# Two of three down-projection parts of a feed-forward block as seven half-sized products

## The chip, the core and the metric

The kernel runs on one core of a Trainium2 chip. The core's engines run side by side, each in the order of its own list of instructions, and wait for one another through semaphores: TensorE (PE) for matrix products, VectorE (DVE) for elementwise work and reductions, ScalarE (ACT) for activations and copies, GpSimd (POOL) and SyncE (SP), which here mostly start transfers. The metric is the device time of one execution in microseconds (us), and the number compared is the median of several runs.

## The reference, cut to what matters

Two layers run one after the other over 512 tokens of width 1024. Each has a token-mixing sublayer and then the feed-forward block that is changed here:

```
def _swiglu(x, w_gate, w_up, w_down):
    h = silu(einsum('bsd,df->bsf', x, w_gate)) * einsum('bsd,df->bsf', x, w_up)
    return einsum('bsf,fd->bsd', h, w_down)

for l in range(2):
    mix = _hybrid_mixer(x, ...)
    x = _layer_norm(ALPHA * x + mix, ln1_g[l], ln1_b[l])
    ffn = _swiglu(x, w_ffn_gate[l], w_ffn_up[l], w_ffn_down[l])
    x = _layer_norm(ALPHA * x + ffn, ln2_g[l], ln2_b[l])
```

The inner width of the block is 2816, that is 22 feature tiles of 128. All arrays are float32.

## The kernel before

**Products in three pieces.** A float32 operand is kept as a high part (a copy that ScalarE rounds to the matmul type) and a low part (the rest, subtracted on VectorE); `hilo` makes the two. Every product of two operands is three matmuls: high by high, high by low, low by high. In the names, `whi` and `wlo` are the parts of a weight, `xh`/`xl` those of the block's input, `ht` those of `h`, `raw` is a weight as loaded, `sn` a working tile, `ps` and `px` are accumulators in PSUM, and `xtok` holds the residual stream of all 512 tokens.

**Seven products instead of eight.** Where two matrices can be cut into 2 by 2 blocks, `tall` and `wide` multiply them by Winograd's form of Strassen's scheme: seven products of half-sized blocks, from sums of blocks of the left side (S1 to S4) and of the right side (P1 to P4). `ORDER` lists the seven as (number, left block, right block). Their results are added in chains of one accumulator: products 1, 6, 7 and 4 go one after the other into chain A, product 2 into chain X, 5 and 3 into chain C. Between two products of a chain the sum so far is read out, because each stage of the chain is a result of its own; the next product may not add to the accumulator before that read. The class `Right` loads the weight blocks; P1 and P3 are made by an accumulating transfer that POOL starts, P2 and P4 by an addition on VectorE in place. Weights' high and low parts lie in two sets of four buffers (`wp`), loaded weights in eight (`rawp`).

**The block before the change.** The 22 feature tiles are worked off in three parts, `FPARTS`, of 6, 8 and 8. In a part, `ffn_plain` (the very first pair) or `ffn_pair` makes two feature tiles of `h` at a time; a pair is seven products of 24 matmuls on 256 columns. Then the part's share of the down projection is added to `xtok`: for each of two halves of 512 output columns, `xstat` runs over the part's feature tiles and four token tiles, three matmuls of 512 columns for each. These are 24 matmuls a feature tile, 528 a layer. Loaded rows of the down weights are split into high and low once and used for all tokens, and `residual` adds each finished accumulator into `xtok`.

**The end of a layer.** In the second half of the last part the four token tiles are taken one after the other (`token_outer`), and `norm` normalizes each as soon as it is complete: statistics, a power on POOL, a refinement, and two passes over 1024 columns on VectorE. In the first layer the normalized tile is also transposed on TensorE (`to_xT`) and split into `xh` and `xl`, which the next layer's first products need; in the second it goes to the output.

**What sets the order.** The program is written as one stream, and a list scheduler orders each engine's instructions by priority and its own guess of when operands are there; pieces of other work are handed in between matmuls by `tick`. Engines then run that fixed order. The order outside the feed-forward block and the first products behind it is the same before and after the change.

Of the kernel before, what the change touches and what calls it, by code (L numbers as in the profile page):

```python
# [11 lines left out]
F32 = mybir.dt.float32  # L12
# [3 lines left out]
ALU = mybir.AluOpType  # L16
# [31 lines left out]
L0, L1 = 383, 255  # L48
WARM = 3
BK = 32  # L50
FPARTS = ((0, 6), (6, 14), (14, 22))


@with_exitstack
def hybrid_kernel(ctx, tc, x, rel_bias, w_in, b_in, w_attn_proj, w_ret_proj, w_out,
# [23 lines left out]
    def stage(name, bufs=1, side="left"):  # L79
        return tc.tile_pool(name=name, bufs=bufs, side=side, reuse_waits="tile")  # L80
# [604 lines left out]
    def layer(ly, cp):  # L685
# [470 lines left out]
        g_, b_ = (fp.tile([P, D], F32, name=n) for n in ("lng", "lnb"))  # L1156
        stats = [sm.tile([P, 2, 6], F32, tag=f"stats{i}", name="stats", bufs=1) for i in range(NI)]

        def ln_par(gsrc, bsrc):
            pool.dma_start(g_, gsrc.partition_broadcast(P))  # L1160
            pool.dma_start(b_, bsrc.partition_broadcast(P))

        def norm(i, dst=None):
            xi = xt[:, i]
            mv = sm.tile([P, 2], F32, tag="mv", name="mv")
            dve.bn_aggr(out=mv, in_=stats[i])
            rs = rstd_of(mv[:, 1:2])
            dve.scalar_tensor_tensor(out=xi, in0=xi, scalar=mv[:, 0:1], in1=g_, op0=ALU.subtract, op1=ALU.mult)
            n = D if dst is None else D // 2
            for c in range(0, D, n):  # L1170
                o_ = xi[:, c:c + n]
                dve.scalar_tensor_tensor(out=o_, in0=o_, scalar=rs, in1=b_[:, c:c + n], op0=ALU.mult, op1=ALU.add)  # L1172
                if dst is not None:
                    nc.sync.dma_start(dst[:, c:c + n], o_)
# [65 lines left out]
        final = ly == DEPTH - 1  # L1240
        cp = []

        def ffn_plain(f, o_):

            ug, uu = pair_units(wg_l, f * P), pair_units(wu_l, f * P)
            pgs = wstat_halves([(u, e) for u in (ug, uu) for e in range(2)])
            drain()
            side.extend(x_sums(xc))
            pace(8)
            for e in range(2):  # L1250
# [3 lines left out]
                hilo(t, o_[:, 0, e], o_[:, 1, e])  # L1254

        def ffn_pair(f, o_):

            sn = {}

            def put(v, ts_):  # L1260
                hilo(v, o_[:, 0, :, ts_], o_[:, 1, :, ts_])

            def ev(i, ps):
                p2 = ps.rearrange("p (q t) -> p q t", q=2)
                if i in (1, 5, 6):
                    sn[i] = work("sn").rearrange("p (q t) -> p q t", q=2)
                    act.copy(out=sn[i], in_=p2)
                elif i == 2:
                    dve.tensor_tensor(out=sn[1], in0=p2, in1=sn[1], op=ALU.add)
                elif i == 3:  # L1270
                    v = sn[6]
                    dve.tensor_tensor(out=v, in0=p2, in1=v, op=ALU.subtract)
                    act.activation(out=v, in_=v, func=AF.Silu)
                    dve.tensor_tensor(out=v, in0=v, in1=sn[1], op=ALU.mult)
                    put(v, slice(0, 256))
                elif i == 7:
                    dve.tensor_tensor(out=sn[5], in0=sn[5], in1=p2, op=ALU.subtract)
# [8 lines left out]
        for part, (f0, f1) in enumerate(FPARTS):  # L1286
            ht = []
            for f in range(f0, f1, 2):
                ht.append(fo.tile([P, 2, 2, S], F32R, tag="op", name="ht"))
                (ffn_pair if f else ffn_plain)(f, ht[-1])  # L1290
                if f == 2:
                    drain()
                    ln_par(ln2_g[ly], ln2_b[ly])

            def h_tok(k, i, ht=ht):
                t, q = ht[k // 2], k % 2
                return t[:, 0, q, i * P:(i + 1) * P], t[:, 1, q, i * P:(i + 1) * P]

            last = part == len(FPARTS) - 1
            rate[0], credit[0] = 0.5 / STEP, 0.0  # L1300
            for hf in range(2):
                def evd(i, ps, hf=hf, part=part, last=last):
                    residual(i, hf, ps, part == 0, last)
                    if last and hf == 1:
# [6 lines left out]
                tail = last and hf == 1  # L1311
# [65 lines left out]
```

## Time and profile before

| | |
|---|---|
| median of three runs | 2134.78 us (2132.10 to 2138.97) |
| the profiled execution, its own time | 2133.13 us |
| its span, first to last instruction | 2131.3 us |
| mean granted TensorE clock | 0.999 |
| busy: PE / DVE / ACT / POOL | 2113.2 / 1488.1 / 1060.9 / 239.5 us |
| down projection, first layer: first matmul on `ht`, first matmul of the last half, last `norm` | 784.6, 1043.8, 1077 us |
| down projection, second layer: first matmul of the last half, last matmul | 2100.4, 2121.9 us |

A row of a timeline gives the start in us, the duration in us, the engine, the line of the program, the operation, the output and inputs with their shapes, how many instructions are merged, and in brackets how long the engine stood idle before it and what ended that. In grouped rows the figures behind the bar are the busy time in us and the mean in ns of one instruction, and then the idle time before them. Matmuls overlap, so the distance from one start to the next, not the duration, is what one costs; VectorE's instructions overlap by less than 0.1 us.

### The profile page before, as it was taken

The numbers are of one execution on the slowest core, as the hardware profiler recorded it, in microseconds if no ns is written. First come the engines' busy times: TensorE is split into PE (matmuls) and PEld (weight loads), VectorE is DVE, ScalarE is ACT, GpSimd is POOL, SyncE is SP. The second block draws the span as 40 slices with busy tenths as digits, with TensorE's granted clock in tenths as the row PEclk, the third lists the DMA queues.
The fourth block names the chain that finished last, engine by engine and source line by source line (L and its number), as shares of the span: only waits on it lengthen the run. The fifth ranks groups of instructions, "written<-read, shape, count | busy, mean of one in ns | idle before, by whom it ended". The sixth has DMA issues, their size and how long they took to land.

```text
span 2131.3 us, 34718 instructions
## 1 busy us (share of the span) xinstructions
PE 2113.2 (99%) x13914; PEld 1917.3 (90%) x13914; DVE 1488.1 (70%) x2113; ACT 1060.9 (50%) x1641; POOL 239.5 (11%) x249
## 2 busy tenths in 40 slices
PE   9999999999999999999999999999999999999998
PEld 8989888889988999989899898888899889999996
DVE  7666888786734776747687578887867358675575
ACT  5567655556623354525255665555665234444350
POOL 4111111101000100000120111101000001010001
PEclk9999999999999999999999999999999999999999
DMA  8866466777776266656258555758687672666551
GB/s 243 213 160 150 124 154 177 181 187 177 242 252 193 60 169 148 168 129 163 76 156 226 144 128 131 194 137 217 158 204 252 211 198 59 179 140 177 120 157 40
DMA packets 313410, 351.32 MB, mean 165 GB/s; under 512 B 22045, under 2 KB 251585, under 8 KB 313120
## 3 DMA queue, kind: packets, MB, share of 16 engines
q1 hardware_dynamic: 227712, 253.01, 38.7%
q0 software_dynamic: 58256, 83.29, 21.1%
q10 hardware_dynamic: 27280, 12.80, 2.1%
q8 instruction: 109, 1.79, 0.3%
q14 instruction: 53, 0.43, 0.1%
HBM read 323.26 MB, written 28.53 MB: 165 GB/s over the span
## 4 chain that ended last, share of the span: by engine, by line
PE 89%; issue 4%; DVE 3%; ACT 2%; DMA 1%; POOL 1%; POOLq 0%; DVEq 0%; ACTq 0%
PE ps L83 81%; PE px L83 6%; DVE wlo L359 1%; PE px L584 1%; PE px L1042 1%; ACT whi L353 1%; ACT s L574 1%; DMA exd<-pk 1%; PE px L192 1%; POOL ry L134 0%; DVE xtok L1172 0%; DMA raw<-in_w_in 0%; DVE raw L375 0%; PE px L649 0%; DMA mb<-exd 0%
## 5 line engine op out<-in xcount | busy, mean ns | idle before, releaser
L359 DVE TENSOR_TENSOR wlo<-raw,whi 128x1024 fp32r<-128x1024 f32 (+1 forms) x462 | 536.8, 1165 | 267.0 <-ACT whi L353 262.5
L353 ACT CAST whi<-raw 128x1024 fp32r<-128x1024 f32 (+1 forms) x462 | 460.7, 1002 | 461.8 <-PE ps L83 252.0
L83 PE MATMUL ps<-xs,whi 128*128 128x256 f32 (+1 forms) x2944 | 572.2, 293 | 0.4 <-ACT sn L814 0.4
L83 PEld LDWEIGHTS ps<-xs,whi 128*128 128x128 f32 x2944 | 467.5, 191 | 15.1 <-issue 1.7
L83 PE MATMUL ps<-xs,wlo 128*128 128x256 f32 (+1 forms) x1472 | 430.2, 292 | 0.6 <-DVE wlo L359 0.6
L83 PE MATMUL ps<-xh,whi 128*128 128x256 f32 (+1 forms) x1424 | 422.7, 299 | 1.9 <-ACT xh L94 1.4
L83 PE MATMUL ps<-xh,wlo 128*128 128x256 f32 (+1 forms) x1424 | 418.6, 295 | 1.0 <-DVE wlo L95 1.0
L83 PE MATMUL ps<-xl,whi 128*128 128x256 f32 (+1 forms) x1424 | 419.5, 295 | 0.0
L83 PEld LDWEIGHTS ps<-xs,wlo 128*128 128x128 f32 x1472 | 281.7, 191 | 6.1 <-DVE wlo L359 1.1
L83 PEld LDWEIGHTS ps<-xh,whi 128*128 128x128 f32 x1424 | 271.0, 191 | 15.3 <-ACT xh L94 2.8
L83 PEld LDWEIGHTS ps<-xl,whi 128*128 128x128 f32 x1424 | 272.2, 191 | 8.3 <-DVE xl L95 0.6
L83 PEld LDWEIGHTS ps<-xh,wlo 128*128 128x128 f32 x1424 | 271.9, 191 | 7.5 <-DVE wlo L95 1.2
L95 DVE TENSOR_TENSOR wlo<-raw,whi 128x1024 fp32r<-128x1024 f32 (+2 forms) x108 | 125.5, 1163 | 167.8 <-ACT whi L94 167.4
L83 PE MATMUL ps<-whi,xs 128*128 128x512 f32 (+1 forms) x768 | 225.0, 362 | 1.0 <-ACT sn L498 1.0
L94 ACT CAST whi<-raw 128x1024 fp32r<-128x1024 f32 (+2 forms) x108 | 107.8, 1001 | 211.6 <-PE ps L83 137.3
L83 PE MATMUL ps<-whi,ht 128*128 128x512 f32 x576 | 178.4, 389 | 0.0
L344 POOL DMA_DIRECT2D raw<-in_w_in x80 | 98.8, 1261 | 691.1 <-DMA raw<-in_w_in 224.0
L375 DVE TENSOR_TENSOR raw<-raw 128x1024 f32<-128x1024 f32 (+1 forms) x132 | 154.3, 1169 | 7.3 <-DMA raw<-in_w_in 5.0
L83 PEld LDWEIGHTS ps<-whi,xs 128*128 128x128 f32 x768 | 137.8, 188 | 20.5 <-ACT sn L498 1.3
L83 PE MATMUL ps<-wlo,xs 128*128 128x512 f32 (+1 forms) x384 | 138.2, 360 | 0.1
L344 POOL DMA_DIRECT2D raw<-in_w_ffn_gate x40 | 51.8, 1294 | 682.1 <-DMA raw<-in_w_ffn_up 239.3
L83 PEld LDWEIGHTS ps<-whi,ht 128*128 128x128 f32 x576 | 108.1, 188 | 22.4
(207 smaller groups left out, 2895.3 us busy)
## 6 DMA issues: line engine op xcount, KB each, us to landing
raw<-in_w_in SPq DMA_DIRECT2D x168, 512.0 KB, 5.3
raw<-in_w_in POOLq DMA_DIRECT2D x64, 512.0 KB, 8.3
raw<-in_w_ffn_up SPq DMA_DIRECT2D x64, 512.0 KB, 4.1
raw<-in_w_ffn_gate SPq DMA_DIRECT2D x44, 512.0 KB, 4.7
raw<-in_w_ffn_down SPq DMA_DIRECT2D x44, 512.0 KB, 3.9
raw<-in_w_ffn_gate POOLq DMA_DIRECT2D x40, 512.0 KB, 6.7
raw<-in_w_ret_proj SPq DMA_DIRECT2D x32, 512.0 KB, 6.3
raw<-in_w_in SPq DMA_DIRECT2D x56, 256.0 KB, 4.8
```

Source lines behind the costliest of these rows:

```text
L83: pe.matmul(ps, lhsT=a, rhs=b, start=start, stop=stop, skip_group_check=True)
L94: act.copy(out=hi, in_=src)
L95: dve.tensor_tensor(out=lo, in0=src, in1=hi.bitcast(F32), op=ALU.subtract)
L192: pe.transpose(px[:, d * P:(d + 1) * P], src[:, (4 * hf + d) * P:(4 * hf + d + 1) * P], ident)
L344: pool.dma_start(r, self.src({"P1": "B12", "P3": "B22"}[n], u), accum_op=ALU.add)
L353: act.copy(out=h, in_=src)
L359: dve.tensor_tensor(out=l, in0=src, in1=h.bitcast(F32), op=ALU.subtract)
L375: dve.tensor_tensor(out=r, in0=r, in1=self.t["B22" if n == "P2" else "B21", u], op=ALU.add)
L574: act.activation(out=s[:, hh, n0:], in_=s[:, hh, n0:], func=AF.Exp, bias=m_, scale=-1.0, accum_out=l_)
L584: pe.transpose(px[:, hh, j * P:(j + 1) * P], ss[od][:, hh, j * P:(j + 1) * P], ident)
L1042: pe.transpose(px[:, t * P:(t + 1) * P], ys[i][:, t * P:(t + 1) * P], ident)
```

## The change

`FPARTS` becomes 8, 8 and 6. The down projection of the first two parts is done by `tall` in its seven-product form (`down_blocks`): the left blocks are `h` with 256 tokens by the four even or four odd feature tiles, the right blocks are the down weights of the even or odd tiles by 512 columns. Tokens are stationary and weights stream, as before. Each product has two token tiles, four feature tiles and three matmuls of 512 columns, which makes 24, and 168 a part. The last part, of six tiles, keeps the old form.

For that, `h` is stored as seven blocks (A11, A12, A22, S1 to S4) with high and low parts. `h_sums` makes S1 to S4 for each pair of feature tiles by four additions of 256 columns on VectorE. A part's 14 pieces of the right side have a high copy and a low subtraction each, four additions for P2 and P4, and four accumulating transfers for P1 and P3; the ten loads and those four transfers stand where eight loads stood. Products 5, 6 and 7 are copied out of PSUM on ScalarE and then added to `xtok`, the others are added from PSUM: 14 additions a part where there were eight. The layer norm's scale and shift lie in other tiles, and those of the second norm are loaded after the last pair.

```diff
-FPARTS = ((0, 6), (6, 14), (14, 22))
+FPARTS = ((0, 8), (8, 16), (16, 22))
+HB = {"A11": 0, "A12": 1, "A22": 2, "S2": 3, "S3": 4, "S4": 5, "S1": 6}
...
-        fo = fin.enter_context(stage("fo", 5))
+        fo = fin.enter_context(stage("fo", 4))
...
+        def h_put(o_, v, c, step):
+            e = c + step * (v.shape[1] - 1) + 1
+            hilo(v, o_[:, c:e:step, 0], o_[:, c:e:step, 1])
+
+        def h_sums(o_, a11, a12, a21, a22):
+            h_put(o_, a22.unsqueeze(1), HB["A22"], 1)
+            dve.tensor_tensor(out=a22, in0=a21, in1=a22, op=ALU.subtract)
+            dve.tensor_tensor(out=a21, in0=a11, in1=a21, op=ALU.subtract)
+            dve.tensor_tensor(out=a11, in0=a22, in1=a11, op=ALU.subtract)
+            dve.tensor_tensor(out=a12, in0=a11, in1=a12, op=ALU.add)
...
-                    put(v, slice(256, 512))
+                    if sums:
+                        h_sums(o_, v0[:, 0], v0[:, 1], v[:, 0], v[:, 1])
+                        h_put(o_, v, HB["S3"], 2)
+                        h_put(o_, v0, HB["S2"], 2)
+                    else:
+                        h_put(o_, v, 2, 1)
...
+        def down_blocks(f0, f1, ht, first):
+            nk = (2,) * ((f1 - f0) // 4)
+
+            def src(b, u):
+                k = f0 + (b[1] == "2") + 4 * u
+                c = (b[2] == "2") * 512
+                return wd_l[:, k:k + 3:2, c:c + 512]
+
+            def left(an, j, ts_):
+                t = ht[j][:, HB[an], :, ts_]
+                return t[:, 0], t[:, 1]
...
+            def ev(i, a, ps):
+                v = ps
+                if i in (5, 6, 7):
+                    v = work("sn")
+                    act.copy(out=v, in_=ps)
...
+            run(tall(Right(src, [(n, 512) for n in nk]), 512, left, ev))
...
+            if not last:
+                down_blocks(f0, f1, ht, part == 0)
+                continue
+            lt = fo.tile([P, 2 * D], F32, tag="op", name="lnp")
+            ln_par(lt, ln2_g[ly], ln2_b[ly])
```

**VectorE at the start of a part's down projection.** In the first layer, changed kernel, from the last instruction that needs the last product of the pair (L1301): `ht_8099` is the part's last pair, `wlo_8374` a low part of the second product's weights, `wlo_8407` and `wlo_8410` those of the third, `ps_8376` and `ps_8390` the two halves of chain A.

```order
L1301 TENSOR_TENSOR sn_8176<-sn_8176,ps_8119 128x512
L360 TENSOR_TENSOR wlo_8374<-raw_8344,whi_8373 128x1024
L96 TENSOR_TENSOR ht_8099<-sn_8206,ht_8099 128x2x256
L96 TENSOR_TENSOR ht_8099<-sn_8176,ht_8099 128x256
L1255 TENSOR_TENSOR sn_8176<-sn_8176 128x256
L1328 SCALAR_TENSOR_TENSOR xtok_6427<-xtok_6427,ps_8376 128x512
L1256 TENSOR_TENSOR sn_8176<-sn_8206,sn_8176 128x256
L1257 TENSOR_TENSOR sn_8206<-sn_8176,sn_8206 128x256
L1258 TENSOR_TENSOR sn_8206<-sn_8206 128x256
L360 TENSOR_TENSOR wlo_8407<-raw_8346,whi_8406 128x1024
L96 TENSOR_TENSOR ht_8099<-sn_8176,ht_8099 128x2x256
L96 TENSOR_TENSOR ht_8099<-sn_8206,ht_8099 128x2x256
```

Before, only two subtractions for `ht` and three weight parts stood between L1281 (the same instruction as L1301) and the first addition to `xtok`; now the sums stand there, and one addition to `xtok` is among them.

**ScalarE inside a part's down projection.** Changed kernel, from the casts of the fourth product's weights on; `ps_8448` and `ps_8464` are the halves of chain C, `ps_8376` and `ps_8390` those of chain A.

```order
L354 CAST whi_8445<-raw_8360 128x1024
L1336 COPY sn_8461<-ps_8448 128x512
L354 CAST whi_8484<-raw_8346 128x1024
L1336 COPY sn_8477<-ps_8464 128x512
L354 CAST whi_8487<-raw_8349 128x1024
L354 CAST whi_8516<-raw_8352 128x1024
L354 CAST whi_8519<-raw_8355 128x1024
L1336 COPY sn_8534<-ps_8376 128x512
L354 CAST whi_8558<-raw_8346 128x1024
L1336 COPY sn_8550<-ps_8390 128x512
L354 CAST whi_8561<-raw_8349 128x1024
L1336 COPY sn_8576<-ps_8376 128x512
```

The copies out of PSUM, which the next product of a chain waits for, stand between casts that wait for weight buffers.

**VectorE at the end of the first layer.** The end of the third token tile's normalization and the fourth's, with the parts that the next layer's first products need (`xl` from the transposed second tile, `wlo` from the next layer's weights). Before:

```order
L1172 SCALAR_TENSOR_TENSOR xtok_6427<-xtok_6427,ry_10654,lnb_6429 128x1024
L95 TENSOR_TENSOR xl_80<-px_10683,xh_79 128x4x128
L1181 TENSOR_TENSOR xtok_6427<-xtok_6427,ps_10664 128x512
L95 TENSOR_TENSOR wlo_10744<-raw_10737,whi_10743 128x1024
L95 TENSOR_TENSOR xl_80<-px_10697,xh_79 128x4x128
L1183 BN_STATS stats_6433<-xtok_6427 128x6
L95 TENSOR_TENSOR wlo_10748<-raw_10740,whi_10747 128x1024
```

Changed:

```order
L1184 TENSOR_TENSOR xtok_6427<-xtok_6427,ps_10778 128x512
L138 TENSOR_TENSOR ry_10768<-ry_10768,rt_10769 128x1
L1186 BN_STATS stats_6431<-xtok_6427 128x6
L1175 SCALAR_TENSOR_TENSOR xtok_6427<-xtok_6427,ry_10768,lnp_10555 128x1024
L1169 BN_AGGR mv_10815<-stats_6431 128x2
L96 TENSOR_TENSOR xl_80<-px_10880,xh_79 128x4x128
L134 TENSOR_SCALAR ve_10817<-mv_10815 128x1
L1171 SCALAR_TENSOR_TENSOR xtok_6427<-xtok_6427,mv_10815,lnp_10555 128x1024
L136 SCALAR_TENSOR_TENSOR rt_10819<-ry_10818,ve_10817 128x1
L96 TENSOR_TENSOR wlo_10852<-raw_10845,whi_10851 128x1024
L137 TENSOR_SCALAR rt_10819<-rt_10819 128x1
L96 TENSOR_TENSOR xl_80<-px_10888,xh_79 128x4x128
```

The fourth tile's addition, statistics and first pass now stand ahead of both `xl` of the second tile and of the first `wlo`. On TensorE a token tile now has 18 matmuls in this loop instead of 24.

More of the change, by code (lines that the diff above doesn't have):

```diff
@@ L1155, in layer, with ln_par @@
         xt = fp.tile([P, NI, D], F32, name="xtok")
-        g_, b_ = (fp.tile([P, D], F32, name=n) for n in ("lng", "lnb"))
+        lnp = []
         stats = [sm.tile([P, 2, 6], F32, tag=f"stats{i}", name="stats", bufs=1) for i in range(NI)]
-        def ln_par(gsrc, bsrc):
-            pool.dma_start(g_, gsrc.partition_broadcast(P))
-            pool.dma_start(b_, bsrc.partition_broadcast(P))
+        def ln_par(t, gsrc, bsrc):
+            lnp[:] = [t[:, n * D:(n + 1) * D] for n in range(2)]
+            for o_, src in zip(lnp, (gsrc, bsrc)):
+                pool.dma_start(o_, src.partition_broadcast(P))
         def norm(i, dst=None):
             xi = xt[:, i]
+            g_, b_ = lnp
             mv = sm.tile([P, 2], F32, tag="mv", name="mv")
@@ L1190, in layer @@
             pool.dma_start(xt, res.rearrange("(i p) d -> p i d", p=P))
-            ln_par(ln1_g[ly], ln1_b[ly])
+            ln_par(mp.tile([P, 2 * D], F32, name="lnp"), ln1_g[ly], ln1_b[ly])
             def wr_unit(dp, h):
@@ L1249, in ffn_plain @@
             pace(8)
+            ts = []
             for e in range(2):
@@ L1253, in ffn_plain, with ffn_pair @@
                 dve.tensor_tensor(out=t, in0=t, in1=pgs[2 + e], op=ALU.mult)
-                hilo(t, o_[:, 0, e], o_[:, 1, e])
-        def ffn_pair(f, o_):
+                h_put(o_, t[:, :256].unsqueeze(1), HB[("A11", "A12")[e]], 1)
+                ts.append(t.rearrange("p (q t) -> p q t", q=2))
+            t0, t1 = ts
+            h_sums(o_, t0[:, 0], t1[:, 0], t0[:, 1], t1[:, 1])
+            h_put(o_, t1, HB["S4"], 1)
+            h_put(o_, t0, HB["S2"], 1)
+        def ffn_pair(f, o_, sums):
             sn = {}
-            def put(v, ts_):
-                hilo(v, o_[:, 0, :, ts_], o_[:, 1, :, ts_])
             def ev(i, ps):
@@ L1274, in ev @@
                     dve.tensor_tensor(out=v, in0=v, in1=sn[1], op=ALU.mult)
-                    put(v, slice(0, 256))
+                    h_put(o_, v, 0, 1)
                 elif i == 7:
@@ L1279, in ev @@
                 elif i == 4:
-                    v = sn[5]
+                    v, v0 = sn[5], sn[6]
                     dve.tensor_tensor(out=v, in0=v, in1=p2, op=ALU.mult)
-                    put(v, slice(256, 512))
-            wide(pair_right(wu_l, wg_l, f * P, WIDE1 if f == 2 else WIDE), x_left, ev)
+                    if sums:
[4 more added lines that the diff above has]
+                        h_put(o_, v, 2, 1)
@@ new lines, in ffn_pair, with add @@
+            wide(pair_right(wu_l, wg_l, f * P, WIDE1 if f == 2 else WIDE), x_left, ev)
+        def down_blocks(f0, f1, ht, first):
[7 more added lines that the diff above has]
+                return t[:, 0], t[:, 1]
+            def add(i, hf, v, fresh, op=ALU.add):
+                o_ = xt[:, i, hf * 512:(hf + 1) * 512]
+                if first and fresh:
+                    dve.scalar_tensor_tensor(out=o_, in0=o_, scalar=ALPHA, in1=v, op0=ALU.mult, op1=op)
+                else:
+                    dve.tensor_tensor(out=o_, in0=o_, in1=v, op=op)
+            def ev(i, a, ps):
[3 more added lines that the diff above has]
+                    act.copy(out=v, in_=ps)
+                if i in (1, 2):
+                    add(a, 0, v, i == 1)
+                elif i == 4:
+                    add(2 + a, 0, v, True)
+                elif i == 5:
+                    add(2 + a, 1, v, True)
+                elif i == 7:
+                    add(2 + a, 1, v, False, ALU.subtract)
+                elif i == 6:
+                    add(a, 1, v, True, ALU.subtract)
+                else:
+                    add(a, 1, v, False)
+            run(tall(Right(src, [(n, 512) for n in nk]), 512, left, ev))
@@ L1286, in layer @@
         for part, (f0, f1) in enumerate(FPARTS):
+            last = part == len(FPARTS) - 1
             ht = []
             for f in range(f0, f1, 2):
-                ht.append(fo.tile([P, 2, 2, S], F32R, tag="op", name="ht"))
-                (ffn_pair if f else ffn_plain)(f, ht[-1])
+                ht.append(fo.tile([P, 7, 2, 256], F32R, tag="op", name="ht"))
+                if f:
+                    ffn_pair(f, ht[-1], not last)
+                else:
+                    ffn_plain(f, ht[-1])
@@ L1291, in layer @@
                 if f == 2:
                     drain()
[L1293 to L1299, printed above, removed]
-            rate[0], credit[0] = 0.5 / STEP, 0.0
+            rate[0], credit[0] = 0.5 / STEP, 0.0
+            if not last:
+                down_blocks(f0, f1, ht, part == 0)
+                continue
@@ L1301, in layer, with h_tok, evd @@
+            lt = fo.tile([P, 2 * D], F32, tag="op", name="lnp")
+            ln_par(lt, ln2_g[ly], ln2_b[ly])
+            def h_tok(k, i):
+                t, q = ht[k // 2], 2 * (i // 2) + k % 2
+                cs = slice(i % 2 * P, (i % 2 + 1) * P)
+                return t[:, q, 0, cs], t[:, q, 1, cs]
             for hf in range(2):
-                def evd(i, ps, hf=hf, part=part, last=last):
-                    residual(i, hf, ps, part == 0, last)
-                    if last and hf == 1:
+                def evd(i, ps, hf=hf):
+                    residual(i, hf, ps, False, True)
+                    if hf == 1:
@@ L1310, in layer @@
                 raws = [load(wd_l[:, a:a + 2, hf * 512:(hf + 1) * 512], 2, 512) for a in range(f0, f1, 2)]
-                tail = last and hf == 1
+                tail = hf == 1
                 if tail and not final:
```

## The prediction

> **What bounds the kernel now.** First the page's busy times and the chain that ended last, then the waits of TensorE, first and last row of nine:
>
> ```profile
> PE 2113.2 (99%) x13914; PEld 1917.3 (90%) x13914; DVE 1488.1 (70%) x2113; ACT 1060.9 (50%) x1641; POOL 239.5 (11%) x249
> PE 89%; issue 4%; DVE 3%; ACT 2%; DMA 1%; POOL 1%; POOLq 0%; DVEq 0%; ACTq 0%
> PE px L83 <- DVE warm L832: 1.5, 1, 1.5
> PE ps L83 <- DVE sn L1277: 0.2, 1, 0.2
> ```
>
> TensorE works all the time and hardly waits; at nine rows of 1.5 us at most, its waits hold nearly nothing. So a removed matmul is worth its distance to the next, wherever nothing else becomes late. Two timeline rows inside a down projection, 17 groups of three apart, give that distance; the grouped rows and the timeline give the counts.
>
> ```profile
> 924.19 0.62 PE L83 MATMUL ps<-whi,ht 128*128 128x512 f32 x2
> 935.75 0.62 PE L83 MATMUL ps<-whi,ht 128*128 128x512 f32 x2
> L83 PE MATMUL ps<-whi,ht 128*128 128x512 f32 x576 | 178.4, 389 | 0.0
> L83 PE MATMUL ps<-wlo,ht 128*128 128x512 f32 x288 | 112.1, 389 | 0.0
> 2100.41 21.92 PE L83 MATMUL ps<-xs,ht 128*128 128x512 f32 x96
> ```
>
> 11.56 us by 51 matmuls is 0.227 us each. There are 864 down matmuls ahead of the last half's token loops and 96 in each loop, 1056 in all. The Trainium skill (TensorE: Matmul & The Clock Gate, section Back-to-back issue gap) gives some 131 ns for a sustained 512-column matmul; by it 96 fewer would save 12.6 us. The trace has 227 ns, and the sum goes by it.
>
> **Matmuls removed.** 24 a feature tile before. After, 168 instead of 192 in each of two parts: 48 fewer a layer, 96 in all, 21.8 us. Where they fall matters. Call T the first matmul of a layer's token loop. Ahead of T there were (6+8+4)x24 = 432 a layer, now 168+168+72 = 408: 24 fewer, 5.44 us. The other 24 come out of the loop itself, since its part has six tiles instead of eight: 18 matmuls a token, 4.08 us instead of 5.44.
>
> **The loop's end, second layer.** VectorE there, the first addition of each token tile and the last pass:
>
> ```profile
> 2106.05 0.69 DVE L1181 TENSOR_TENSOR xtok<-xtok,ps 128x512 f32<-128x512 f32 x1 [2.53 <-PE ps L83]
> 2111.51 0.68 DVE L1181 TENSOR_TENSOR xtok<-xtok,ps 128x512 f32<-128x512 f32 x1
> 2116.95 0.68 DVE L1181 TENSOR_TENSOR xtok<-xtok,ps 128x512 f32<-128x512 f32 x1
> 2122.40 0.68 DVE L1181 TENSOR_TENSOR xtok<-xtok,ps 128x512 f32<-128x512 f32 x1
> 2126.51 1.42 DVE L1172 SCALAR_TENSOR_TENSOR xtok<-xtok,ry,lnb 128x512 f32<-128x512 f32 x2
> ```
>
> Only the first waits for TensorE; then a tile takes VectorE 5.45 us, as long as its 24 matmuls. The norm doesn't shrink. With 4.08 us a tile, the first starts 1.36 us earlier after T and the rest keep 5.45 us. So 1.36 of 5.44 us arrive.
>
> **The loop's end, first layer.** VectorE and then TensorE before; T is 1043.84:
>
> ```profile
> 1043.84 15.12 PE L83 MATMUL ps<-xs,ht 128*128 128x512 f32 x66
> 1049.48 0.69 DVE L1181 TENSOR_TENSOR xtok<-xtok,ps 128x512 f32<-128x512 f32 x1 [2.54 <-PE ps L83]
> 1054.91 0.69 DVE L1181 TENSOR_TENSOR xtok<-xtok,ps 128x512 f32<-128x512 f32 x1
> 1060.26 0.69 DVE L95 TENSOR_TENSOR xl<-px,xh 128x512 fp32r<-128x512 f32 x1
> 1060.86 0.68 DVE L1181 TENSOR_TENSOR xtok<-xtok,ps 128x512 f32<-128x512 f32 x1
> 1064.81 0.22 DVE L135 SCALAR_TENSOR_TENSOR rt<-ry,ve 128x1 f32<-128x1 f32 x1 [0.46 <-POOL ry L134]
> 1065.45 1.29 DVE L1172 SCALAR_TENSOR_TENSOR xtok<-xtok,ry,lnb 128x1024 f32<-128x1024 f32 x1
> 1066.65 0.68 DVE L95 TENSOR_TENSOR xl<-px,xh 128x512 fp32r<-128x512 f32 x1
> 1067.85 1.22 DVE L95 TENSOR_TENSOR wlo<-raw,whi 128x1024 fp32r<-128x1024 f32 x1
> 1068.98 0.68 DVE L95 TENSOR_TENSOR xl<-px,xh 128x512 fp32r<-128x512 f32 x1
> 1065.18 0.60 PE L192 MATMUL px<-ident,xtok 128*128 128x128 f32 x4
> 1065.54 1.64 PE L83 MATMUL ps<-xs,ht 128*128 128x512 f32 x6
> 1069.12 0.38 PE L83 MATMUL ps<-xh,wlo 128*128 128x256 f32 x1 [0.97 <-DVE wlo L95]
> ```
>
> TensorE went on at T+25.3, after 0.97 us of waiting for the next layer's first `wlo`. After the change it has 72 matmuls (16.3 us) and four groups of transposes (0.38 each) and is ready at T+17.9. VectorE, in the new order: first tile at T+4.28, two tiles of 5.43 and 5.35: T+15.06. To L136 of the third tile the same 3.95 us as 1060.86 to 1064.81: T+19.0. Then 0.64 of refinement with an `xl`, the fourth tile's addition and its statistics between (0.60 each): T+21.45; the last pass 1.20; statistics, the second tile's first `xl` and L134 0.9: T+23.5. Its first pass with the power 1.73, then 0.14: T+25.4. The first `wlo` 1.13: T+26.5; the second `xl` at T+27.3 and the second `wlo` at T+28.5. TensorE thus idles 5.3 us for the first `xl`, 2.7 for the first `wlo`, 0.6 for the second: it passes the same point at T+27.1, **1.8 us later** after T than before. Of this loop's 5.44 us nothing arrives.
>
> **VectorE under the pairs.** A steady pair, and the stage of values and gates, which is the same seven products of 24 matmuls on 512 columns (columns: us, then busy time and count of PE, PEld, DVE, ACT, POOL, clock, DMA share, GB/s); then prices:
>
> ```profile
> 961.70:981.90 20.20, 20.20 (x171) 20.20 (x170) 15.18 (x17) 10.94 (x15) 3.86 (x3) 1.00 0.78 183
> 444.00:482.00 38.00, 38.00 (x191) 32.01 (x190) 29.60 (x39) 24.95 (x36) 3.87 (x4) 1.00 0.78 194
> 427.13 0.68 DVE L739 TENSOR_TENSOR sn<-sn,ps 128x512 f32<-128x512 f32 x1
> 427.73 0.42 DVE L712 TENSOR_TENSOR sn<-sn,rs 128x256 f32<-128x256 f32 x1
> 428.07 0.42 DVE L713 TENSOR_TENSOR sn<-sn,rs 128x256 f32<-128x256 f32 x1
> L359 DVE TENSOR_TENSOR wlo<-raw,whi 128x1024 fp32r<-128x1024 f32 x14 | 17.1, 1222 | 8.1 <-ACT whi L353 8.1
> ```
>
> From start to start 512 columns cost VectorE 0.60 us, 256 cost 0.34. A pair with sums has five pieces of 256 more (four sums, A22) and one of 512: 2.3 us on top of 15.2 in 20.2. Here 8.1 us in two pairs were idle ahead of `wlo`, waiting for a buffer to come free: it fills that. Cost 0; without the cover 2.3 us for each of 16 pairs. ScalarE's casts (10.9 of 20.2) fit likewise.
>
> **VectorE in the seven products.** A part is 168 matmuls, 38.1 us. VectorE has 14 `wlo` and four sums of weights at about 1.14 us (1.22 less the overlap) and 14 additions at 0.60: 28.9 us. The values stage had 29.6 busy in 38 and TensorE full, with the same ten loads and four accumulating transfers behind a pair, in the same eight buffers; so DMA, POOL's queue and VectorE's share cost 0 here. At its start, V being the end of the pair's last product: L1301 ends at V+0.8; the `wlo` waits for its cast, whose buffer that product held, until V+1.1, and ends at V+2.3; the low part of the last pair's A11 at V+2.95. TensorE's order puts the matmul that needs it behind 13 others, V+2.95. The sums' low parts are there at V+7.7, wanted at V+10.9. I take 0.1 us a part, bounds 0 and 0.5, four parts. At the first pairs of a layer VectorE has no idle time: that is the 0.2 us wait for L1277 in the list above. There the 2.3 us of new pieces come ahead of L1277, but in the new order a `wlo` and an `ht` piece (1.7 us) that stood ahead of it come behind; I take 0.1 us more a layer, bounds 0 and 1.2.
>
> **Sum.** -5.44 - 1.36 in the second layer, -5.44 + 1.8 in the first, +0.6: -9.9 us. Against the execution's own 2133.1 us that is 2123.3; the median of three stands 1.65 us above, so **2125 us**.
>
> **Rivals.** *The clock falls in the gap.* The end of the kernel, last matmul at 2122.3, TensorE's granted clock in the column behind the count:
>
> ```profile
> 2126.00:2127.00 1.00, 0.00 (x0) 1.00 0.00 0
> 2127.00:2128.00 1.00, 0.00 (x0) 0.59 0.00 0
> 2128.00:2129.00 1.00, 0.00 (x0) 0.50 0.89 332
> ```
>
> After 5.1 us of idleness the clock fell to half. The gap above is 5.3 us, then 2.7 more behind three matmuls. How long it stays down with work no row shows; between at once and the 5.1 us that it took to fall, the loss lies between 0 and 2.6 us. With 2.4: 2127.3 us. Against it: the gap is at the edge, and part of the slow matmuls falls into waits. The Trainium skill (TensorE: Matmul & The Clock Gate, Part 1: The HAM clock gate) says half rate comes after one idle window of 3.4 us and full rate after one busy one; the window runs freely, so a gap of 5.3 us may hold one or not; the trace's 5.1 us agrees with it.
>
> *Reads of a chain come late.* Products 5, 6 and 7 must be copied out of PSUM on ScalarE before the next product adds to the same accumulator: three changes a part, 12 in all. A half's copy has the other half's 12 matmuls, 2.72 us. If a cast ahead of it in ScalarE's queue waits for a buffer that only the running product frees, the change waits for cast and copy:
>
> ```profile
> L353 ACT CAST whi<-raw 128x1024 fp32r<-128x1024 f32 x406 | 423.2, 1047 | 430.4 <-PE ps L83 230.5 <-issue 104.0 <-DVE raw L375 56.7
> L1267 ACT COPY sn<-ps 128x512 f32<-128x512 f32 x60 | 34.9, 582 | 4.1 <-PE ps L83 4.1
> ```
>
> 1.05 + 0.58 and 0.2 of signals, 1.8 us by 12 is 22 us: 2147. For it speaks that 230 us of cast idleness ends on a released buffer; against it, that with two buffers a product the casts ahead of a copy want buffers freed a product earlier. It decides above 0.28 us a change (no difference that can be told) and above 1.35 (slower).
>
> *All 96 count.* If the loops' ends hide in something, 2134.8 - 21.8 = 2113. The unbroken 5.45 us steps speak against it.
>
> **How the numbers follow.** About 0.3%, 6.4 us, is what can be told from no change. Forecast 0.45 (own range 2122 to 2128); clock 0.19, of it 0.15 faster; late reads 0.10 slower and 0.20 within; all 96 0.06. Faster 0.66, same 0.24, slower 0.10. The range, 2118 to 2133: below, a shorter gap at the layers' border (up to 4 us) and the spread of three runs; above, the part starts' bounds (2 us), the clock and 0.3 us a change.
>
> **What would show it.** 960 down matmuls, at 0.227 us; TensorE idle some 8 us once, behind the first layer, on `xl` and `wlo`; second layer's tiles at 5.45 us steps from T+4.3; no waits of TensorE on L1336, L1328 or `ht` above 0.5 us; pairs still 20.2 us apart. Waits at each product change, or pairs longer than 20.2, would prove it wrong.

## The result, and the profile after

The changed kernel takes **2124.62 us** (median of 6, 2120.86 to 2126.33), the kernel before in the same session 2134.60 (median of 6, 2131.61 to 2138.97): a ratio of 0.995 with a 95% interval of 0.9936 to 0.9965, or 7.5 to 13.7 us less. Predicted were 2125 us, range 2118 to 2133. The profiled execution's own time is 2125.37 us, its span 2123.3.

The page of the changed kernel, its groups of down matmuls (busy us and mean ns behind the first bar), and the two longest waits of TensorE (us in total, times, longest):

```profile
PE 2096.5 (99%) x13818; PEld 1902.2 (90%) x13818; DVE 1585.6 (75%) x2275; ACT 1112.6 (52%) x1723; POOL 258.3 (12%) x265
...
L84 PE MATMUL ps<-whi,ht 128*128 128x512 f32 x544 | 169.1, 390 | 0.0
L84 PE MATMUL ps<-wlo,ht 128*128 128x512 f32 x272 | 105.9, 389 | 0.0
L84 PE MATMUL ps<-xs,ht 128*128 128x512 f32 x144 | 33.5, 391 | 0.0
PE ps L84 <- ACT whi L95: 4.0, 1, 4.0
PE ps L84 <- DVE wlo L96: 2.1, 1, 2.1
```

There are 960 down matmuls, 96 fewer. TensorE is busy 16.7 us less, VectorE 97.5 us more, and the two waits, once each, are new.

Single executions of one kernel differ by 2 to 9 us, more than most effects here. Stretches between fixed matmuls inside the traces are steadier. The marks, from TensorE's timeline (in its rows the moving operand stands first behind the arrow): **F** is the first `ps<-xs,whi` matmul of a layer's first `ffn_pair`, **T** the first matmul of the token loop as in the prediction, **B** the first such `xs` matmul of the second layer. Before F, B and F of the second layer (both T before stand in the prediction), then all five marks after (the duration and count of a T row end with the view's window):

```profile
749.58 0.40 PE L83 MATMUL ps<-xs,whi 128*128 128x256 f32 x2
1100.02 0.40 PE L83 MATMUL ps<-xs,whi 128*128 128x256 f32 x2
1806.33 0.40 PE L83 MATMUL ps<-xs,whi 128*128 128x256 f32 x2
```

```profile
749.74 0.40 PE L84 MATMUL ps<-xs,whi 128*128 128x256 f32 x2
1039.03 6.28 PE L84 MATMUL ps<-xs,ht 128*128 128x512 f32 x27
1097.70 0.40 PE L84 MATMUL ps<-xs,whi 128*128 128x256 f32 x2
1805.43 0.40 PE L84 MATMUL ps<-xs,whi 128*128 128x256 f32 x2
2094.42 7.87 PE L84 MATMUL ps<-xs,ht 128*128 128x512 f32 x34
```

| stretch | before, us | after, us | difference | predicted |
|---|---|---|---|---|
| first layer, F to T | 294.26 | 289.29 | -4.97 | -5.14 |
| layers' border, T to B | 56.18 | 58.67 | +2.49 | +1.8 |
| second layer ahead of F, B to F | 706.31 | 707.73 | +1.42 | 0 |
| second layer, F to T | 294.08 | 288.99 | -5.09 | -5.14 |
| second layer, T to the span's end | 30.89 | 28.88 | -2.01 | -1.36 |

The four stretches that the change touches give -9.6 us where the steps gave -9.8. The stretch from B to F, whose instructions the change leaves in their order, gives 1.4 back in this one execution; where, stands in the last section.

**The border.** TensorE there after the change, VectorE, and then windows (the number behind the counts is the granted clock):

```profile
1056.28 1.04 PE L193 MATMUL px<-ident,xtok 128*128 128x128 f32 x8
1061.35 0.38 PE L84 MATMUL ps<-xh,whi 128*128 128x256 f32 x1 [4.03 <-ACT whi L95]
1062.06 0.53 PE L84 MATMUL ps<-xl,whi 128*128 128x256 f32 x1 [0.32 <-DVE ve L134]
...
1065.12 0.58 PE L84 MATMUL ps<-xh,wlo 128*128 128x256 f32 x1 [2.10 <-DVE wlo L96]
...
1068.70 0.41 PE L84 MATMUL ps<-xh,whi 128*128 128x256 f32 x1
1068.91 0.31 PE L84 MATMUL ps<-xl,whi 128*128 128x256 f32 x1
```

```profile
1058.73 0.68 DVE L1184 TENSOR_TENSOR xtok<-xtok,ps 128x512 f32<-128x512 f32 x1
...
1061.98 1.28 DVE L1171 SCALAR_TENSOR_TENSOR xtok<-xtok,mv,lnp 128x1024 f32<-128x1024 f32 x1
...
1063.85 1.22 DVE L96 TENSOR_TENSOR wlo<-raw,whi 128x1024 fp32r<-128x1024 f32 x1
...
1065.71 1.22 DVE L96 TENSOR_TENSOR wlo<-raw,whi 128x1024 fp32r<-128x1024 f32 x1
```

```profile
1056.00:1061.00 5.00, 1.32 (x10) 0.94 (x9) 4.51 (x10) 3.28 (x6) 1.52 (x1) 1.00 0.16 64
1063.00:1068.00 5.00, 2.90 (x14) 2.88 (x14) 4.54 (x8) 3.04 (x4) 0.68 (x1) 0.50 0.53 183
1069.00:1070.00 1.00, 1.00 (x10) 1.00 (x10) 1.00 (x2) 0.00 (x0) 0.97 (x2) 1.00 0.79 271
```

VectorE works 4.5 of 5 us; the fourth token tile's addition and first pass stand ahead of the first `wlo`, which ends at T+26.0. TensorE stands idle until T+22.3, for a moment until T+23.0, and again until T+26.1. Its clock falls to half, and some 18 matmuls follow 0.21 us apart instead of 0.12.

**The end.** VectorE's first additions of the four token tiles in the second layer's loop, and the last pass:

```profile
2098.70 0.69 DVE L1184 TENSOR_TENSOR xtok<-xtok,ps 128x512 f32<-128x512 f32 x1 [1.17 <-PE ps L84]
...
2104.17 0.68 DVE L1184 TENSOR_TENSOR xtok<-xtok,ps 128x512 f32<-128x512 f32 x1
...
2108.16 0.68 DVE L1184 TENSOR_TENSOR xtok<-xtok,ps 128x512 f32<-128x512 f32 x1
...
2112.97 0.68 DVE L1184 TENSOR_TENSOR xtok<-xtok,ps 128x512 f32<-128x512 f32 x1
...
2118.24 1.42 DVE L1175 SCALAR_TENSOR_TENSOR xtok<-xtok,ry,lnp 128x512 f32<-128x512 f32 x2
```

The first stands at T+4.28, as predicted. From it to the last pass it takes 19.54 us, where it took 20.46 before: VectorE still sets the pace, but the distances between these additions are 5.47, 3.99 and 4.81 us.

### The profile page after: what moved, and what is told of

The parts are those of the page before. It is cut to its first block, busy times and chain, and to the rows that moved or that the text cites. A ratio compares the mean times of both kernels' runs of the same rounds, so it can differ in the third digit from the quotient of the medians.

```text
span 2123.3 us, 34880 instructions
## 1 busy us (share of the span) xinstructions
PE 2096.5 (99%) x13818; PEld 1902.2 (90%) x13818; DVE 1585.6 (75%) x2275; ACT 1112.6 (52%) x1723; POOL 258.3 (12%) x265
## 4 chain that ended last, share of the span: by engine, by line
PE 88%; issue 4%; DVE 3%; DMA 2%; ACT 2%; POOL 1%; SPq 0%; POOLq 0%; DVEq 0%; ACTq 0%
PE ps L84 80%; PE px L84 6%; DMA raw<-in_w_in 1%; DVE wlo L360 1%; PE px L585 1%; PE px L1043 1%; ACT whi L354 1%; POOL ry L135 1%; DMA y_d<-yt 0%; PE px L193 0%; ACT s L575 0%; DVE xtok L1175 0%; PE px L650 0%; DMA exd<-pk 0%; DVE raw L376 0%
## 5 line engine op out<-in xcount | busy, mean ns | idle before, releaser
L354 ACT CAST whi<-raw 128x1024 fp32r<-128x1024 f32 (+1 forms) x518 | 519.6, 1008 | 461.8 <-PE ps L84 190.0
L360 DVE TENSOR_TENSOR wlo<-raw,whi 128x1024 fp32r<-128x1024 f32 (+1 forms) x518 | 604.7, 1171 | 207.9 <-ACT whi L354 202.1
L84 PEld LDWEIGHTS ps<-xh,whi 128*128 128x128 f32 x1424 | 272.2, 192 | 19.2 <-ACT whi L95 4.9
L96 DVE TENSOR_TENSOR wlo<-raw,whi 128x1024 fp32r<-128x1024 f32 (+2 forms) x78 | 88.8, 1140 | 125.1 <-ACT whi L95 125.0
L376 DVE TENSOR_TENSOR raw<-raw 128x1024 f32<-128x1024 f32 (+1 forms) x148 | 173.9, 1175 | 8.8 <-DMA raw<-in_w_in 6.7
L84 PE MATMUL ps<-whi,ht 128*128 128x512 f32 x544 | 169.1, 390 | 0.0
L95 ACT CAST whi<-raw 128x1024 fp32r<-128x1024 f32 (+2 forms) x78 | 76.4, 982 | 142.8 <-PE ps L84 100.3
L84 PEld LDWEIGHTS ps<-whi,ht 128*128 128x128 f32 x544 | 101.8, 188 | 22.4 <-DVE ht L96 1.5
```

The costliest lines, as they stand in the source:

```text
L84: pe.matmul(ps, lhsT=a, rhs=b, start=start, stop=stop, skip_group_check=True)
L95: act.copy(out=hi, in_=src)
L96: dve.tensor_tensor(out=lo, in0=src, in1=hi.bitcast(F32), op=ALU.subtract)
L354: act.copy(out=h, in_=src)
L360: dve.tensor_tensor(out=l, in0=src, in1=h.bitcast(F32), op=ALU.subtract)
L376: dve.tensor_tensor(out=r, in0=r, in1=self.t["B22" if n == "P2" else "B21", u], op=ALU.add)
```

## The experiments

The theory: a removed matmul brings its 0.227 us where it lies ahead of T, and inside a token loop only as far as VectorE doesn't bound the loop. The rivals: all 96 bring the same; the reads of a chain are late; the sums cost VectorE time that shows; the fallen clock costs at the border.

The measured numbers of all kernels, by the touched stretches (F to B in the first layer, F to the end in the second) of one profiled execution each, and by medians:

| kernel | F to B | F to end | sum | against before | median, us | ratio to before, 95% |
|---|---|---|---|---|---|---|
| before | 350.44 | 324.97 | 675.41 | | 2134.78 | |
| the change | 347.96 | 317.87 | 665.83 | -9.6 | 2124.62 | 0.9936 to 0.9965 |
| order_alone | 359.00 | 328.00 | 687.00 | +11.6 | 2144.30 | 1.0032 to 1.0057 |
| one_part | 345.22 | 319.87 | 665.09 | -10.3 | 2120.90 | 0.9927 to 0.9954 |
| keep_clock | 347.80 | 317.90 | 665.70 | -9.7 | 2121.21 | 0.9933 to 0.9958 |
| keep_clock_30 | 346.98 | 317.85 | 664.83 | -10.6 | 2125.17 | 0.9936 to 0.9969 |
| no_sums | 348.06 | 318.12 | 666.18 | -9.2 | 2125.35 | 0.9944 to 0.9969 |
| more_copies | 347.75 | 317.85 | 665.60 | -9.8 | 2127.04 | 0.9955 to 0.9981 |
| loop_24 | 344.08 | 317.64 | 661.72 | -13.7 | 2121.88 | 0.9931 to 0.9968 |
| loop_30 | 339.38 | 314.63 | 654.01 | -21.4 | 2113.91 | 0.9885 to 0.9919 |

Each ratio is to the runs of the kernel before on the same chip (medians 2134.30 us for order_alone, one_part, keep_clock and no_sums, 2133.08 for the other four). Medians stray from the stretches by up to 4 us, both ways, so the stretches decide where less than that is at stake.

### Where a matmul lies: the order of the parts alone, and one part alone

```diff
 # order_alone: parts 8, 8, 6, all in the old form
+            blocked = False
...
-                    ffn_pair(f, ht[-1], not last)
+                    ffn_pair(f, ht[-1], blocked)
...
-            if not last:
+            if blocked:
                 down_blocks(f0, f1, ht, part == 0)
                 continue
```

> The parts are 8, 8 and 6 tiles as in the change, but all three are projected in the old form: 1056 down matmuls, as before, of which 72 instead of 96 lie in each layer's token loop and 456 instead of 432 ahead of it (T is the loop's first matmul). No sums of h. Theory (a matmul counts only where it lies ahead of T): 24 more ahead of T are 5.44 us a layer, 10.9 in all; the border between the layers costs 3.9 us more behind T, as the trace after shows (1.8 forecast plus the fallen clock); the second layer's loop gives back 1.36 and 0.9 us. Together about 12 us slower than before (11 to 13), 2147 us. Rival (all matmuls count alike, and the order of the parts is free): 2134.6 us, no change.

```diff
 # one_part: seven products in the first part only, eight tiles in the token loop
-FPARTS = ((0, 8), (8, 16), (16, 22))
+FPARTS = ((0, 8), (8, 14), (14, 22))
...
+            blocked = part == 0
...
-            if not last:
+            if blocked:
                 down_blocks(f0, f1, ht, part == 0)
                 continue
```

> Only the first part, of eight tiles, is projected as seven products; then a part of six and one of eight tiles follow in the old form, so that the token loop keeps 24 matmuls a token. 1008 down matmuls, 48 fewer than before and 48 more than after the change. Theory: all 24 removed matmuls of a layer lie ahead of T, the layers' border and the end are as before: 2 x (5.44 - 0.1 to 0.4 at the part's start) = 10.1 to 10.7 us faster than before, 2124.2 us, so as fast as the change with half of its saving. At the border no wait above 1.1 us, the clock stays at 1.00. Rival (the 96 removed matmuls brought their 10 us evenly): half of it, 2129.6 us.

The order alone, with the 1056 matmuls of the kernel before, makes the kernel slower: ratio 1.0045 (1.0032 to 1.0057), +10.0 us by medians and +11.6 by stretches, where 11 to 13 were expected. F to T is 5.43 and 5.34 us longer in the two layers, which is 24 matmuls each; T to B is 3.1 us longer (3.9 expected), with the waits of the change; T to the end 2.3 us shorter. The rival "no change" falls.

In `one_part` the later two parts keep only four blocks of `h` a pair, in a pool of their own. With one part in seven products only 48 matmuls are saved instead of 96, and the kernel is as fast as the change: 0.9941 (0.9927 to 0.9954), -10.3 us by stretches where the change has -9.6. F to T is 5.20 and 5.30 us shorter, T to B 56.16 us against 56.18, T to the end 31.1 against 30.9. TensorE's waits at the border, first with the order alone, then with one part:

```profile
PE ps L84 <- ACT whi L95: 4.0, 1, 4.0
PE ps L84 <- DVE wlo L96: 2.1, 1, 2.1
```

```profile
PE ps L84 <- DVE wlo L96: 1.0, 1, 1.0
...
PE ps L84 <- ACT whi L95: 0.6, 1, 0.6
```

In `one_part` the granted clock stays at 1.00 here. So the waits belong to the loop of 18 matmuls, not to the products. The second 48 removed matmuls bring the change nothing beyond what the one part has.

### The sums of h

```diff
 # no_sums
-HB = {"A11": 0, "A12": 1, "A22": 2, "S2": 3, "S3": 4, "S4": 5, "S1": 6}
+HB = {"A11": 0, "A12": 1, "A22": 3, "S2": 0, "S3": 1, "S4": 3, "S1": 2}
...
-                    ffn_pair(f, ht[-1], not last)
+                    ffn_pair(f, ht[-1], False)
```

> The changed kernel without the sums of h: each pair stores four blocks instead of seven, and the products that want S1 to S4 read one of the four blocks in their place, so this leaves out the part of the computation that makes S1 to S4 (four additions and their casts and low parts a pair, 16 pairs). All matmuls stay. Theory (that work lies in VectorE's idle time ahead of wlo, and only the starts of four parts show it): 0.2 to 1.2 us shorter than the change, 2123.9 us; a pair still takes 20.2 us. Rival (pairs or parts wait for VectorE in more places than the list of waits tells): 2.3 us for each pair that has no cover, so 5 us or more.

Four pairs of the first layer's second part with the sums, then the part's down projection, and the four pairs without the sums (columns: us, then PE, PEld, DVE, ACT, POOL):

```profile
843.21:923.85 80.64, 80.64 (x674) 80.63 (x673) 66.42 (x80) 45.70 (x61) 10.05 (x8) 1.00 0.75 180
923.85:962.21 38.36, 38.36 (x171) 31.47 (x170) 33.95 (x41) 19.22 (x24) 5.07 (x4) 1.00 0.78 198
```

```profile
841.78:922.42 80.64, 80.64 (x674) 80.63 (x673) 59.30 (x62) 42.93 (x55) 11.24 (x9) 1.00 0.74 181
```

VectorE works 7.1 us less in four pairs, and the pairs take the same 80.64 us. The sums are hidden entirely. My expectation that their absence shortens the parts' starts was wrong: F to T is 289.37 us without them and 289.29 with. A down projection takes 38.36 us, 0.2 to 0.3 more than 168 matmuls at 0.227, with or without sums; in both traces the weight load at the part's start waits 0.4 us for the last pair's own low part.

### Reads of a chain

```diff
 # more_copies
                 if i in (5, 6, 7):
                     v = work("sn")
                     act.copy(out=v, in_=ps)
+                    for _ in range(2):
+                        act.copy(out=work("sn"), in_=ps)
```

> The changed kernel with each of the 24 copies out of PSUM (products 5, 6 and 7) made three times, the two more into working tiles that nobody reads: the read that the next product of the chain waits for ends 1.16 us later. Theory (a half's read has the other half's 12 matmuls, 2.72 us, and ends 2.0 us ahead of need): nothing, 0 +- 1 us against the change. The rival that I gave a chance of 0.30 (reads come late) would cost 0.58 to 1.16 us at each of 12 changes: 7 to 14 us.

F to T stays 289.28 and 289.01 us, T to the end 28.84. Three copies instead of one change nothing in any stretch that holds them, so a read is at least 1.16 us early. ScalarE's waits for TensorE in the changed kernel's first layer tell the same (us in total, times, longest):

```profile
ACT sn L1336 <- PE ps L84: 10.6, 12, 1.6
```

All 12 copies of the layer waited for TensorE, so none of them was held up by a cast ahead of it. The median of 8 runs is 2.4 us above the change's, outside the expected 1 us, with intervals that overlap; in the profiled execution the touched stretches are no longer, and what the median adds is not explained.

### The clock at the border

```diff
 # keep_clock; keep_clock_30 has range(30)
             need(2 * t, 2 * t + 1)
+            if keep_clock and t == 0:
+                px = psum()
+                for _ in range(20):
+                    mm(px, xs[:, 0, 0, 0, :P], xs[:, 0, 0, :2].rearrange("p a b -> p (a b)"), True, True)
```

> The changed kernel with 20 matmuls of 512 columns more in the gap at the layers' border, behind the transposes of the last token tiles and ahead of the next layer's first product; their result is read by nobody. They take 20 x 0.227 = 4.5 us of the 4.7 us in which TensorE stood idle. Theory (the idle gap lowers the clock, and that costs 18 matmuls 0.09 us each, less the second wlo's wait that comes out of hiding): the granted clock stays at 1.00 at the border, and the time is 1.1 to 1.7 us shorter than after the change, some 2123.2 us. Rival (the slow matmuls lie in waits anyway, or the clock falls for another reason): no difference from the change, 2124.6 us, or 0.3 us longer.

With 20 the experiment didn't do what it was for. Its T is 1041.37; TensorE after the unread matmuls, and then a window:

```profile
1064.73 0.28 PE L84 MATMUL ps<-xl,whi 128*128 128x256 f32 x1
1067.46 0.39 PE L84 MATMUL ps<-xh,wlo 128*128 128x256 f32 x1 [2.45 <-DVE rt L137]
```

```profile
1068.00:1070.00 2.00, 2.00 (x12) 2.00 (x11) 2.00 (x4) 1.53 (x2) 0.00 (x0) 0.51 0.66 154
```

TensorE worked on the unread matmuls until T+22.7 and on the first products until T+23.6; then it waited 2.45 us for the first `wlo`, and at T+26.7 the clock fell all the same. T to B is 58.47 us, 0.2 less than with the change. The median is 3.4 us below the change's; the profiled execution is the slowest of the five, 2126.99 us, and the others have no trace, so whether their borders were shorter isn't shown. So the gap was filled further:

> The changed kernel with 30 instead of 20 unread matmuls in the border's gap, so that TensorE is busy until 1.1 us before the first low part of the weights is there (T+26.1). With 20 the clock fell at T+26.7 all the same, for 3.2 us, behind the 2.45 us wait for that part. Theory: the clock stays at 1.00, the 15 matmuls that ran at half rate there take 1.4 us less, and the stretch from T to the second layer's first matmul on sums is 57.1 us (56.8 to 57.7) instead of 58.67 after the change and 58.47 with 20. Rival (what is left is VectorE's lateness, and the slow matmuls lay in it): 58.3 us or more. The whole time moves by too little to tell.

```profile
1067.00:1069.00 2.00, 1.83 (x16) 1.63 (x15) 2.00 (x3) 0.76 (x1) 0.11 (x1) 1.00 0.80 258
1069.00:1072.00 3.00, 3.00 (x28) 3.00 (x27) 1.87 (x2) 0.00 (x0) 2.08 (x4) 1.00 0.95 290
```

Here the clock holds 1.00 throughout the border, and T to B is 57.66 us, at the upper end of what was expected: 1.0 less than with the change, 1.5 more than before. The first matmul on `wlo` starts at T+26.1 in both, so the 1.0 us lies behind it, where the changed kernel's clock is down and this one's isn't. So of the 2.5 us lost at the border the clock takes 1.0 and VectorE's lateness 1.5, of it 0.8 at the first `wlo` (T+25.3 before). As expected, the whole time shows nothing of it.

### A loop that VectorE doesn't bound

If the loop of 18 matmuls is too short for VectorE, more of the last part's matmuls should stand in it. `loop_30` and `loop_24` compute the same 960 products; only the order of the last part's 144 matmuls differs.

```diff
 # loop_30; loop_24 has range(4) and range(4, 6)
+            pss = [psum("ps") for _ in range(NI)]
+            for j in range(2):
+                for i in range(NI):
+                    one(pss[i], 0, j, i)
+            for i in range(NI):
+                for j in range(2, 6):
+                    one(pss[i], 0, j, i)
+                evd(i, 0, pss[i])
+                ps = psum("ps")
+                for j in range(6):
+                    one(ps, 1, j, i)
+                evd(i, 1, ps)
```

> The changed kernel with another last part: of its 36 matmuls a token tile, only the first two feature tiles of the first column half run ahead for all token tiles; the other 30 (four feature tiles of the first half, all six of the second) are taken token by token. 960 down matmuls as after the change, in the same products. A token tile's matmuls take 30 x 0.227 = 6.81 us; VectorE has its 5.45 us and one more addition with statistics (1.2), 6.65 us. Theory (a removed matmul counts unless VectorE bounds the loop; here the matmuls do): both layers get nearly all of the 48: 10.9 less 0.5 for the part starts, less 0 to 1.5 for the tight VectorE, each: 18 to 20.8 us faster than before, 2114.5 us. The stretch from T to the second layer's first matmul on sums then has no idle time above 2 us and the clock stays at 1.00. Rival (the norm's chain sets each loop's end whatever the matmuls do): as after the change, 2124.6 us.

> As the kernel with 30 matmuls a token tile in the loop, but four feature tiles of the first half run ahead and 24 matmuls a token tile are in the loop: 5.44 us, against the 6.65 us that VectorE needs now for a tile. Same 960 matmuls. Theory: VectorE bounds the loop, three steps of 1.2 us a layer are lost against the loop of 30: 3.6 us a layer, 7.2 in all, so 11 to 14 us faster than before, 2121.5 us; the first additions of the second layer's tiles stand 6.6 us apart. Rival (the end depends on the number of matmuls alone): like the loop of 30.

`loop_30` beats both kernels: 2113.91 us, ratio to the kernel before 0.9902 (0.9885 to 0.9919). That is 19.2 us by medians; the four stretches give -21.4 us, against 21.8 for 96 matmuls and 18 to 20.8 expected. VectorE in its second layer (the additions that end a token tile, and the last pass), and TensorE at the border:

```profile
2088.84 0.69 DVE L1184 TENSOR_TENSOR xtok<-xtok,ps 128x512 f32<-128x512 f32 x1 [0.24 <-PE ps L84]
...
2095.64 0.69 DVE L1184 TENSOR_TENSOR xtok<-xtok,ps 128x512 f32<-128x512 f32 x1 [0.26 <-PE ps L84]
...
2102.44 0.69 DVE L1184 TENSOR_TENSOR xtok<-xtok,ps 128x512 f32<-128x512 f32 x1 [0.26 <-PE ps L84]
...
2106.56 1.42 DVE L1175 SCALAR_TENSOR_TENSOR xtok<-xtok,ry,lnp 128x512 f32<-128x512 f32 x2
```

```profile
1057.28 0.39 PE L84 MATMUL ps<-xh,wlo 128*128 128x256 f32 x1 [0.33 <-DVE wlo L96]
```

Now each of these additions waits 0.25 us for TensorE: the steps are 6.80 us, 30 matmuls. At the border the waits are 0.3 us and the clock stays at 1.00. In `loop_24` only the first of these additions waits; the first and the last of the four:

```profile
2089.49 0.69 DVE L1184 TENSOR_TENSOR xtok<-xtok,ps 128x512 f32<-128x512 f32 x1 [2.66 <-PE ps L84]
...
2108.70 0.68 DVE L1184 TENSOR_TENSOR xtok<-xtok,ps 128x512 f32<-128x512 f32 x1
```

Three steps take 19.21 us, 6.40 each where I expected 6.6, and 24 matmuls take 5.44. It loses 7.7 us to `loop_30` by stretches (7.2 expected), 8.0 by medians: 3.0 us in the second layer, where 3.6 were expected, and 4.7 in the first, where TensorE waits 2.4 us for a weight cast at the border and the clock falls for 3.4 us besides. The number of matmuls is the same in both, so the rival that the number alone decides falls. The kernel before with a loop of 30 wasn't run. What the new loop could bring there without fewer matmuls can only be estimated: TensorE waited 0.97 us at the border before, and its last matmul ended 9 us ahead of the end, as in `loop_30`, so about 1 of the 21.4 us at most.

## Why the prediction came out right, point by point

- **Pitch and count.** 960 matmuls at 0.227 us, shown by F to T, 5.43 us for 24 more in `order_alone`, and by `loop_30`, which gets 21.4 us out of 96. The Trainium skill's 131 ns for a sustained 512-column matmul (TensorE: Matmul & The Clock Gate, section Back-to-back issue gap) would have made that 12.6; the runs disagree with it for these operands.
- **24 of 48 a layer ahead of T: -5.44 each.** Shown, at -4.97 and -5.09 with the part starts.
- **Part starts 0.1 us each.** Mis-sized: 0.2 to 0.3 each, by the 38.36 us of a part, inside the bounds of 0 and 0.5. What is late is what the prediction named, the last pair's own low part, and not the sums.
- **Pairs at no cost.** Shown: 80.64 us for four with and without the sums.
- **The layers' first pairs, 0.1 each.** No wait of that kind stands out in the trace; too small to tell.
- **"1.36 of 5.44 arrives" in the second layer.** The mechanism was right: VectorE sets the pace and the first addition stands at T+4.28. The step "the rest keep 5.45" was wrong: in the new order the additions of the last two tiles stand inside the norm of the tile before instead of behind it. Where another tile's instruction stands between two that depend on each other, their distance shrinks: from the second addition to the next instruction it is 0.72 us, from the third 0.60. These places make up the 0.92 us from the first addition to the last pass. The stretch behind the last pass is 0.3 us longer, so 2.0 us arrive instead of 1.36.
- **"1.8 us later" at the first layer's border.** Lateness 1.5 us, by keep_clock_30. The times were near, one cause was missing: the long wait ended at T+22.3 with the cast of the first weights, on ScalarE behind copies that waited for VectorE; the first `xl` let the next matmul go at T+23.0, forecast at T+23.2, and the first `wlo` at T+26.1, forecast at T+26.5. The second `wlo` shows as a wait in keep_clock_30 alone, 0.17 us; with the change the slow clock hides it.
- **The clock rival, given 0.19.** Its event happened in the profiled execution. Its price was 1.0 us instead of 2.4, since part of the slow matmuls lay in waits, as the prediction had held against it. How long the clock stays down, which no row showed then, was 6.8 us. So the forecast's case without the clock isn't what ran; that the time fits so closely is luck, since this 1.0 us was nearly made up by 0.65 more at the end and 0.3 less lateness.
- **Late reads, given 0.30.** Didn't happen: the copies waited for their products and not behind casts, and more_copies shows a reserve of at least 1.16 us a read. The 0.2 us of signals in this rival's price was read from no row; after the end of a `wlo` TensorE went on within 0.05 us (1065.07 to 1065.12).
- **The sum.** Its terms give -9.84 us, not -9.9; the forecast is the same.
- **All 96 count, given 0.06.** Not with the loop of 18; with the loop of 30 nearly all do. The reason that the prediction gave against it, the unbroken VectorE steps, is what that loop removes.

## What to carry to other kernels

A removed instruction of the busiest engine is worth its pitch only where that engine sets the pace: split the program into its stretches, and ask of each who would be late if this engine were faster. A loop at the end that another engine just keeps up with takes back what is saved in it, so move work into that loop until the busy engine bounds it again: here 96 fewer matmuls brought 10 us in one order and about 20 in another, against the same kernel before. Where executions differ by more than the effect, compare distances between the same two instructions in the traces.

## What the runs showed of the hardware that was not expected

The clock falls sooner than the prediction's 5.1 us at the kernel's end suggested (its rows give 4.9). In keep_clock 2.45 us of waiting behind 0.9 us with four matmuls brought it to half. In the second layer's attention, where the change leaves the order as it was, TensorE has a place with two short waits; the changed kernel there:

```profile
1205.00:1207.00 2.00, 0.76 (x7) 0.55 (x5) 1.96 (x8) 0.50 (x4) 0.00 (x0) 1.00 0.00 0
1207.00:1209.00 2.00, 1.39 (x9) 1.02 (x10) 2.00 (x6) 1.77 (x8) 0.00 (x0) 0.98 0.00 0
1209.00:1211.00 2.00, 2.00 (x11) 1.60 (x12) 1.46 (x3) 1.41 (x3) 0.00 (x0) 0.50 0.00 0
```

With 2.15 us of work in 4 us the clock fell for 3.4 us. The amount of work alone doesn't decide it. At the same place, first no_sums with 2.45 us of work in 4 and what followed, then loop_24 with 2.05 and what followed:

```profile
1204.00:1208.00 4.00, 2.45 (x17) 1.88 (x16) 3.88 (x11) 2.56 (x9) 0.00 (x0) 0.94 0.00 0
1208.00:1212.00 4.00, 4.00 (x25) 3.32 (x24) 3.59 (x9) 1.85 (x6) 0.00 (x0) 0.63 0.01 1
```

```profile
1200.00:1204.00 4.00, 2.05 (x12) 1.50 (x10) 2.58 (x10) 2.16 (x6) 0.61 (x1) 1.00 0.06 1
1204.00:1208.00 4.00, 3.68 (x31) 3.20 (x32) 3.46 (x4) 2.56 (x7) 0.00 (x0) 1.00 0.00 0
```

What the traces share is a beat. Every change of the granted clock in one execution lies a whole number of times 3.413 us from every other: in the changed kernel at 1062.14, 1068.96, 1208.92, 1212.32 and 2113.44 us, which is 0, 2, 43, 44 and 308 beats behind the first. Falls lasted one beat (keep_clock, loop_24), two (the change's border, 6.8 us) or three (order_alone's, 10.2 us). With the ten traces cut into such beats, behind the first 60 us and up to the last matmul, TensorE was busy for at most 0.54 of a beat that ended in a fall and for at least 0.50 of one that didn't, by the profile's busy time; between the two both occur. So a wait can lower the clock or not by where it lies in the beats, and that differs from one execution to the next.

It fell in the attention in the profiled executions of the change, no_sums, keep_clock_30 and loop_30, and B to F was 707.7 to 709.3 us in these; in before, order_alone and one_part it held, at 706.1 to 706.3. That is where this execution's 1.4 us went, and a part of the spread between executions. It isn't all of it: keep_clock, more_copies and loop_24 had 707.2, 707.9 and 708.1 us without such a fall. The three shortest stretches belong to the three kernels without seven products in a second part; whether the change has a share in this isn't shown. The Trainium skill (TensorE: Matmul & The Clock Gate, Part 1: The HAM clock gate) says that half rate comes after an idle window of about 3.4 us whose position is free. The traces agree with the length and the free position; that the window must be idle they don't bear out, since beats with up to half of work in them ended in a fall.
